# Output of a recurrence kept with its steps on the partitions, its group norm taken along the free axis

## The chip, the cores and the metric

One core of a Trainium2 chip runs the whole program. The metric is the device time of one execution in microseconds (us); a measurement of this kernel can tell about 0.2% (4.7 us) from no change. TensorE does the matrix products, VectorE (DVE in the rows), ScalarE (ACT) and GpSimd (POOL) the rest, SyncE (SP) issues most transfers.

## The reference, cut to what matters

Two layers of a decoder. Every layer has one wide input projection, sliding-window attention on one half of its heads, a recurrence (RWKV-7) on the other half, gates, and an output projection. The change concerns the recurrence's output `ys` for 512 prompt positions and 8 single-step samples, 16 heads of 64 channels:

```python
def step(S, inp):
    r_t, w_t, k_t, v_t, kk_t, a_t = inp
    sa = jnp.einsum('bhij,bhj->bhi', S, -kk_t)
    S = (S * w_t[:, :, None, :] + sa[..., None] * (kk_t * a_t)[:, :, None, :]
         + v_t[..., None] * k_t[:, :, None, :])
    return S, jnp.einsum('bhij,bhj->bhi', S, r_t)
...
mu = jnp.mean(ys, axis=-1, keepdims=True)
var = jnp.mean(jnp.square(ys - mu), axis=-1, keepdims=True)
yn = ((ys - mu) * lax.rsqrt(var + GN_EPS)).reshape(Bn, T, RWKV_WIDTH)
yn = yn * ln_w.astype(f32) + ln_b.astype(f32)
bonus = jnp.sum(r_h * k_h * r_k.astype(f32), axis=-1, keepdims=True) * v_h
y_rw = (yn + bonus.reshape(Bn, T, RWKV_WIDTH)).astype(x.dtype)
```

## The kernel before, in words

All products of a layer form one stream on TensorE: 53 column tiles of the input projection, then 16 of the output projection. A tile takes 96 products of 260 columns (`quarter`, L378; tiles `psP`, `psR`, `psQ`, `psA`, `psO` and so on), each with weights that are split in two parts, `hi` (made on ScalarE, L353) and `lo` (made on VectorE, L363); `lo` is made three quarters of a tile, that is at least 48 products, ahead of its use.

Everything else is written as generators. `Side.tick` is called after each product of the stream and lets at most one generator go on; `yield n` means: go on n products of the stream later. I call the gap between two products of the stream a *place*, and a distance in places is the sum of the numbers that are yielded. So the order of the instructions on every engine is fixed when the program is built, and an engine works through its list strictly from the top.

The recurrence is done by `chain(p, ...)`, once for each of 8 pairs of heads in each of 2 layers, 16 in all; three of them are under way at a time. Its parts, in order:

- the inputs are scaled, and products of queries and keys (`atp`, L636) give the 64x64 matrices `atq`, `atk` of 8 chunks of 64 steps;
- GpSimd inverts 31 steps of triangular 32x32 blocks: it fetches `f` (L660, four transfers) and then does two instructions a step, `tmp` and `xi` (L668, L670);
- blocks are put together: VectorE transposes (`x`, L725), TensorE multiplies them (`t2a`, L731 and L739), with copies by VectorE in between (L734, L743);
- the 8 chunks in turn (tile `seq`): L761 makes both the queries' and the keys' product with the state, of which only the keys' half is read (`rr`, L762); L768 and two copies (`sv`, L769, L770); L772 makes the new state, to which VectorE adds the old one (`mbd`, L779); L773 and L775 add up the output with the channels on the partitions, and ScalarE copies it to `y` (L785);
- the samples' state (`sa`, `st`, `vz`, L793 to L811) and their output (`ys`, L817, L821);
- the group norm of prompt and samples together, over partitions: `y` is split in two parts, a product centres it (`yc`), ScalarE squares it, a second split and product give the variance (`vp`), ScalarE takes the logarithm and the exponential (L840, L841), VectorE scales and adds (L843, L845), the gate `gr` is fetched and multiplied (L849), and the result goes to memory (`yd`, L850).

The tail of pair p runs beside the chunks of pair p+1 and the inversion of pair p+2.

## Time and profile before

| | |
|---|---|
| three runs | 2343.62, 2343.07, 2341.40 us; median 2343.07 |
| the profiled execution | 2344.84 us, of which the span of its instructions is 2343.1 us |
| TensorE, products | busy 2220.5 us of the span, 95% |
| VectorE | busy 1482.1 us, 63% |
| ScalarE | busy 1057.8 us, 45% |
| GpSimd | busy 790.9 us, 34% |
| mean granted TensorE clock | 0.979 of full speed |

The profiled execution lies 1.8 us above the median, and 1.7 us of it lie outside the span. A busy share is an average; TensorE's busy time counts overlapping products once.

### The profile page before, as it was taken

Reading aid. Unit: us, or ns where it says so; the run is one execution under the profiler, and the core shown is the slowest. Engines: PE = TensorE matmul, PEld = TensorE weight load, DVE = VectorE, ACT = ScalarE, POOL = GpSimd, SP = SyncE. Lnnn points to the kernel's source line nnn. Section 1 sums busy time; section 2 is a strip of 40 time slices with the busy share of each in tenths; the row PEclk is TensorE's granted clock in tenths of the full one; section 3 lists DMA queues with packets and bytes.
Section 4 is the critical chain, followed back from the end, with each engine's and each line's share of the span. In section 5 each row is a group of like instructions: output and inputs, shape, how many; then the busy total and the mean of one; then the engine's idle time right before and its main releaser. Section 6 shows DMA issues by size and latency. Waiting matters only on the chain.

```text
span 2343.1 us, 53879 instructions
## 1 busy us (share of the span) xinstructions
PE 2220.5 (95%) x20708; PEld 2094.3 (89%) x20708; DVE 1482.1 (63%) x3712; ACT 1057.8 (45%) x2346; POOL 790.9 (34%) x1412
## 2 busy tenths in 40 slices
PE   5999999999999999999999999999999999999997
PEld 3889989999989898899989998989999999889997
DVE  3465676767885886533376456577766778765445
ACT  3344355545454556422245345344554546553222
POOL 1005656666567000000021516655676430000112
PEclk8999999999999999999999999999999999999998
DMA  9945555333333225777762445543332332144335
GB/s 343 350 160 162 169 168 159 103 90 96 106 91 102 60 78 161 221 239 247 238 215 77 141 149 177 165 123 106 94 96 85 94 93 76 62 132 135 115 116 177
DMA packets 231393, 337.99 MB, mean 144 GB/s; under 512 B 61760, under 2 KB 82368, under 8 KB 230976
## 3 DMA queue, kind: packets, MB, share of 16 engines
q1 hardware_dynamic: 225248, 321.95, 44.3%
q0 software_dynamic: 5888, 12.59, 1.8%
q8 instruction: 163, 2.67, 0.5%
q14 instruction: 94, 0.77, 0.1%
HBM read 303.97 MB, written 32.56 MB: 144 GB/s over the span
## 4 chain that ended last, share of the span: by engine, by line
PE 71%; DVE 12%; DMA 6%; ACT 4%; issue 3%; POOL 3%; SPq 1%; DVEq 0%; ACTq 0%; POOLq 0%
PE psP L378 17%; PE psO L378 14%; PE psA L378 6%; PE psR L378 6%; PE psQ L378 5%; PE psS L378 4%; PE adps L297 4%; DMA rawa<-in_wada_dram 2%; DVE lo L363 2%; PE psK L378 2%; POOL xi L670 1%; PE atp L636 1%; POOL tmp L668 1%; PE seq L772 1%; DMA raw<-in_wout_dram 1%
## 5 line engine op out<-in xcount | busy, mean ns | idle before, releaser
L363 DVE TENSOR_TENSOR lo<-raw,hi 128x512 fp32r<-128x512 f32 x568 | 414.0, 730 | 454.3 <-PE psO L378 133.5
L353 ACT CAST hi<-raw 128x512 fp32r<-128x512 f32 x568 | 350.5, 618 | 628.4 <-PE psP L378 213.5
L378 PE MATMUL psP<-hh,lo 128*128 128x260 f32 x1408 | 307.5, 292 | 0.0
L378 PE MATMUL psP<-hl,hi 128*128 128x260 f32 x1408 | 304.9, 292 | 0.0
L378 PE MATMUL psP<-hh,hi 128*128 128x260 f32 x1408 | 303.8, 292 | 0.2 <-ACT dm L516 0.2
L670 POOL TENSOR_TENSOR xi<-xi,tmp 128x248 f32<-128x248 f32 (+30 forms) x496 | 283.5, 572 | 38.9
L668 POOL TENSOR_TENSOR tmp<-f,xi 128x248 f32<-128x248 f32 (+30 forms) x496 | 257.6, 519 | 85.2 <-DMA f<-d 47.8
L378 PEld LDWEIGHTS psP<-hh,lo 128*128 128x128 f32 x1408 | 225.6, 192 | 6.0 <-issue 4.1
L378 PEld LDWEIGHTS psP<-hl,hi 128*128 128x128 f32 x1408 | 224.9, 192 | 5.9 <-issue 3.3
L378 PEld LDWEIGHTS psP<-hh,hi 128*128 128x128 f32 x1408 | 224.4, 192 | 3.1 <-issue 1.6
L378 PE MATMUL psO<-yh,hi 128*128 128x260 f32 x1024 | 223.5, 284 | 3.6 <-DVE xsn L1191 3.6
L378 PE MATMUL psO<-yh,lo 128*128 128x260 f32 x1024 | 223.2, 284 | 1.7 <-DVE lo L363 1.7
L378 PE MATMUL psO<-yl,hi 128*128 128x260 f32 x1024 | 222.9, 284 | 0.0
L378 PEld LDWEIGHTS psO<-yh,hi 128*128 128x128 f32 x1024 | 165.0, 189 | 5.7 <-issue 5.6
L378 PEld LDWEIGHTS psO<-yh,lo 128*128 128x128 f32 x1024 | 165.2, 189 | 3.6 <-DVE lo L363 1.9
L443 POOL TENSOR_TENSOR rmsr<-rmsv,mhalf 128x3 f32<-128x3 f32 x6 | 5.6, 939 | 476.6 <-DMA raw<-in_wout_dram 444.1
L378 PEld LDWEIGHTS psO<-yl,hi 128*128 128x128 f32 x1024 | 165.0, 189 | 1.6 <-issue 1.6
L1328 POOL TENSOR_SCALAR yo<-xnew,fg 128x260 f32<-128x260 f32 x32 | 31.2, 978 | 392.1 <-DVE xnew L1188 367.9
L297 PE MATMUL adps<-rawa,cT 128*32 128x128 f32 (+1 forms) x2048 | 116.8, 347 | 29.6 <-DMA rawa<-in_wada_dram 29.3
L785 ACT COPY y<-seq 64x64 f32<-64x64 f32 x256 | 52.5, 205 | 194.6 <-DVE mbd L779 135.1
L378 PE MATMUL psQ<-hl,hi 128*128 128x260 f32 x512 | 117.6, 295 | 0.0
L297 PEld LDWEIGHTS adps<-rawa,cT 128*32 128x32 f32 x2048 | 55.2, 114 | 67.2 <-DMA rawa<-in_wada_dram 23.1
(361 smaller groups left out, 5499.9 us busy)
## 6 DMA issues: line engine op xcount, KB each, us to landing
raw<-in_win_dram SPq DMA_DIRECT2D x424, 256.0 KB, 3.3
rawa<-in_wada_dram SPq DMA_DIRECT2D x384, 256.0 KB, 5.0
raw<-in_wout_dram SPq DMA_DIRECT2D x152, 256.0 KB, 3.7
f<-d POOLq DMA_DIRECT2D x64, 128.0 KB, 3.3
gd<-th SPq DMA_DIRECT2D x22, 260.0 KB, 2.6
gr<-gd SPq DMA_DIRECT2D x22, 260.0 KB, 3.8
x<-in_xt_dram SPq DMA_DIRECT2D x16, 260.0 KB, 5.2
yd<-rk SPq DMA_DIRECT2D x16, 260.0 KB, 3.5
```

The costliest lines, as they stand in the source:

```text
L297: pe.matmul(ap[32 * g:32 * g + 32, 0:w], cT[:, kk, :], raw[g * w // 512][:, c:c + w], start=(kk == 0), stop=(kk == KT - 1))
L353: se.copy(out=his[n], in_=raws[n])
L363: ve.tensor_tensor(out=lo, in0=raws.pop(n), in1=hi, op=ALU.subtract)
L378: pe.matmul(ps[:, h, 0:NH], a[:, k % 4], b[:, h * NH:(h + 1) * NH], start=(k == k0 and j == 0), stop=stop)
L443: ge.tensor_tensor(out=r[:, 0:3], in0=v[:, 0:3], in1=mhalf[:, 0:3], op=ALU.pow)
L636: pe.matmul(pss[h][:, e, :], kb[g][hs, e].rearrange("p a t -> p (a t)"), qk[g][hs, e].rearrange("p a t -> p (a t)"), start=True, stop=True)
L668: ge.tensor_tensor(out=tv, in0=f[:, s:s + 1, s + 1:32].to_broadcast([128, 8, 31 - s]), in1=xi[:, :, s:s + 1].to_broadcast([128, 8, 31 - s] ...
L670: ge.tensor_tensor(out=xi[:, :, s + 1:32], in0=xi[:, :, s + 1:32], in1=tv, op=ALU.add)
L772: pe.matmul(mn, kbt[g][:, e], sv[g][:, e], start=True, stop=True)
L785: se.copy(out=y[hs, 64 * c:64 * c + 64], in_=yp[hs, h])
L1328: ge.tensor_scalar(out=out[h][m // 2][:, m % 2], in0=xn[:, h * NH:h * NH + NH], scalar1=fg[:, m:m + 1], scalar2=None, op0=ALU.mult)
```

## The change

The line numbers of the changed kernel are those of before plus 2 to 26.

- Output of a chunk: L761's product already holds the queries' half with the steps on the partitions; ScalarE copies it to `yq` (L777 in the changed kernel). The rest of the output is made with `atq` as the weights, one product of 64 columns for each of the two heads (L791), and copied to `y` (L800). L773 and L775 of before are gone. The weights are read 128 columns wide though only 64 of the results are used; for the last head of a group 72 wide. `atq` has 8 columns more for that, which GpSimd clears.
- GpSimd adds `y` and `yq` (L802).
- Group norm of the prompt: the channels of a head now lie along the free axis, so VectorE takes mean and variance with 8 BN_STATS and 8 BN_AGGR (L812, L815), GpSimd makes the factor and the offset (`rs8`, `mv`, L816 to L820, one of them a power), ScalarE applies them in 8 instructions (L842), four transposes on TensorE bring the channels back to the partitions (`yT`, L855), and VectorE scales and adds (L856).
- Samples: the old way, but on 8 columns alone (L861 to L874, with a power on GpSimd, L870, whose result VectorE reads at L872).
- The last instruction also adds `ln_b` (L875). Factors of one half moved into the parameters (`hrk`, `hln`, `lnw4`).
- Distances: 40 more places ahead of the fetch of `f`; 10, 8 and 4 more in the tail; yields with the sum of 101 places are gone with the norm's old steps. `x1` moved to the shared pool `t2`, which has 72 buffers and not 71.

```diff
@@ -586,7 +588,7 @@
             se.activation(out=rn2, in_=rn2, func=AF.Exp, scale=-0.5)
             ve.tensor_tensor(out=k, in0=k, in1=kr, op=ALU.mult)
             rk = t2([128, N], "rk")
-            ve.scalar_tensor_tensor(out=rk, in0=r, scalar=pc(P_RK), in1=k, op0=ALU.mult, op1=ALU.mult)
+            ve.scalar_tensor_tensor(out=rk, in0=r, scalar=hrk[:, l, p:p + 1], in1=k, op0=ALU.mult, op1=ALU.mult)
             yield W[14]
             kk = rn2
             ve.scalar_tensor_tensor(out=kk, in0=kr, scalar=pc(P_KK), in1=rn2, op0=ALU.mult, op1=ALU.mult)
@@ -623,11 +625,15 @@
 
             yield W[23] // 2
             rks = low(rk, rkh)
-            atq, atk = [], []
+            atq, atk, aqs = [], [], []
             flat = lambda ap: ap.rearrange("p e h t -> p (e h) t")
             d1 = dp.tile([2, 16, 32, 32], F32, tag="d1", name="d1")
             for g in range(2):
-                atq.append(t2([128, 4, 2, 64], "atq"))
+
+                aq = t2([128, 520], "atq")
+                ge.memset(aq[:, 512:520], 0.0)
+                aqs.append(aq)
+                atq.append(aq[:, 0:512].rearrange("p (e h t) -> p e h t", e=4, h=2))
                 atk.append(t2([128, 4, 2, 64], "atk"))
                 pss = [ps1("atp").rearrange("p (x t) -> p x t", t=128) for _ in range(2)]
                 for e in range(4):
@@ -656,6 +662,7 @@
                 b = kb[g].rearrange("p e a t -> p e (a t)")
                 ge.tensor_tensor(out=b, in0=b, in1=pend8[:, 4 * g:4 * g + 4].unsqueeze(2).to_broadcast([128, 4, 128]),
                                  op=ALU.mult)
+            yield 40
             for j in range(4):
                 ge.dma_start(out=f[j:128:4], in_=d1.rearrange("b c s t -> (b c) s t"))
             xi = wk.tile([128, 8, 32], F32, tag="xi", name="xi", bufs=1)
@@ -720,7 +727,7 @@
                                  in_=d2[b, 8 * g:8 * g + 8].rearrange("c j t -> j c t"))
             yield W[28]
 
-            x1 = sm.tile([128, 2, 8, 32], F32, tag="x1", name="x1", bufs=1)
+            x1 = t2([128, 2, 8, 32], "x1")
             for i in range(2):
                 ve.transpose(out=x1[64:96, i], in_=flat(xT[i])[64:96, :, 0:32])
             yield W[29]
@@ -742,7 +749,13 @@
                 o = (64, 96)[i]
                 ve.tensor_copy(flat(xT[i])[64:96, :, 32:64], pa[o:o + 32, 8:16])
             yield W[31]
-            y = t2([128, N], "y")
+
+            y = t2([128, 4, 128], "y")
+            yq = t2([128, 4, 128], "yq")
+            ge.memset(yq[0:64, 0], 0.0)
+            st6 = sm.tile([128, 8, 6], F32, tag="st6", name="st6", bufs=2)
+            mv = sm.tile([128, 8, 2], F32, tag="mv", name="mv", bufs=2)
+            rs8 = sm.tile([128, 8], F32, tag="rs8", name="rs8", bufs=2)
             for c in range(8):
                 if c == 6:
                     st = t2([128, B, 64], "st")
@@ -755,11 +768,13 @@
                 m0, m1 = mbd[p % 2][c % 2], mbd[p % 2][1 - c % 2]
                 ps = ps1("seq")
                 rp, sp, mn = ps[:, 0:128], ps[:, 128:256], ps[:, 256:384]
-                yp = ps[:, 384:512].rearrange("p (h t) -> p h t", h=2)
+                ap = ps[:, 384:512]
+                ys = slice(64 * (c % 2), 64 * (c % 2) + 64)
                 rr = rrs[p % 2]
                 if c:
                     pe.matmul(rp, qk[g][:, e].rearrange("p a t -> p (a t)"), m0, start=True, stop=True)
                     ve.tensor_tensor(out=rr[64:128], in0=rp[64:128], in1=sv[g][64:128, e], op=ALU.add)
+                    se.copy(out=yq[ys, c // 2], in_=rp[0:64])
                     yield W[32] + 4
                 else:
                     ve.tensor_copy(rr[64:128], sv[g][64:128, e])
@@ -770,9 +785,11 @@
                 ve.tensor_copy(sv[g][64:128, e, 64:128], sp[64:128, 64:128])
                 yield W[33] + 4
                 pe.matmul(mn, kbt[g][:, e], sv[g][:, e], start=True, stop=True)
-                pe.matmul(yp, sv[g][:, e], atq[g][:, e], start=True, stop=(c == 0))
-                if c:
-                    pe.matmul(yp, m0, qk[g][:, e, 0].unsqueeze(1).to_broadcast([128, 2, 64]), start=False, stop=True)
+                for h in range(2):
+                    o = 128 * e + 64 * h
+                    w = min(128, 520 - o)
+                    pe.matmul(ap[0:w, 64 * h:64 * h + 64], aqs[g][:, o:o + w], sv[g][:, e, 64 * h:64 * h + 64],
+                              start=True, stop=True)
                 for h in range(2):
                     hs = slice(64 * h, 64 * h + 64)
                     if c:
@@ -780,10 +797,9 @@
                                                 in1=mn[hs, hs], op0=ALU.mult, op1=ALU.add)
                     else:
                         ve.tensor_copy(m1[hs, hs], mn[hs, hs])
-                for h in range(2):
-                    hs = slice(64 * h, 64 * h + 64)
-                    se.copy(out=y[hs, 64 * c:64 * c + 64], in_=yp[hs, h])
+                se.copy(out=y[ys, c // 2], in_=ap[0:64])
                 yield W[34]
+            ge.tensor_tensor(out=y, in0=y, in1=yq, op=ALU.add)
             for h in range(2):
                 sy.dma_start(out=o_sp[l, p, 64 * h:64 * h + 64], in_=m1[64 * h:64 * h + 64, 64 * h:64 * h + 64])
 
@@ -791,7 +807,17 @@
             sa = t2([128, B * 64], "sa")
             sb = lambda ap: ap.rearrange("p (b i) -> p b i", b=B)
             ve.tensor_tensor(out=sb(sa), in0=st, in1=bc(smp[:, 1]), op=ALU.mult)
-            yield W[35]
+            yield W[35] + 10
+            for i in range(8):
+                ve.bn_stats(out=st6[:, i], in_=y[:, i // 2, 64 * (i % 2):64 * (i % 2) + 64])
+            yield 8
+            for i in range(8):
+                ve.bn_aggr(out=mv[:, i], in_=st6[:, i])
+            ge.tensor_scalar(out=rs8, in0=mv[:, :, 1], scalar1=GN_EPS, scalar2=None, op0=ALU.add)
+            ge.tensor_tensor(out=rs8, in0=rs8, in1=mhalf, op=ALU.pow)
+            yield 4
+            ge.tensor_tensor(out=mv[:, :, 0], in0=mv[:, :, 0], in1=rs8, op=ALU.mult)
+            ge.tensor_scalar(out=mv[:, :, 0], in0=mv[:, :, 0], scalar1=-1.0, scalar2=None, op0=ALU.mult)
             sah = t2([128, B * 64], "sah", F32R)
             se.copy(out=sah, in_=sa)
             ve.tensor_tensor(out=st, in0=st, in1=bc(smp[:, 5]), op=ALU.mult)
@@ -810,43 +836,43 @@
                                     op1=ALU.mult)
             ve.tensor_tensor(out=st, in0=st, in1=sb(sa), op=ALU.add)
             sy.dma_start(out=o_ss[l, p], in_=st)
+
+            for i in range(8):
+                yi = y[:, i // 2, 64 * (i % 2):64 * (i % 2) + 64]
+                se.activation(out=yi, in_=yi, func=AF.Identity, scale=rs8[:, i:i + 1], bias=mv[:, i, 0:1])
             yield W[38]
             ps = ps1("ys")
 
             for b in range(0, B, 2):
                 pe.matmul(ps[:, 2 * b:2 * b + 4], st[:, b:b + 2].rearrange("p b i -> p (b i)"),
                           rbd[:, b:b + 2].rearrange("p b h -> p (b h)"), start=True, stop=True)
+            ysm = sm.tile([128, 4, B], F32, tag="ysm", name="ysm", bufs=2)
             for h in range(2):
                 for i in range(2):
-                    ve.tensor_copy(y[64 * h:64 * h + 64, T + i:N:2], ps[64 * i:64 * i + 64, 2 * i + h:2 * B:4])
+                    ve.tensor_copy(ysm[64 * h:64 * h + 64, 0, i:B:2], ps[64 * i:64 * i + 64, 2 * i + h:2 * B:4])
+            ps = ps1("yT")
+            for j in range(4):
+                pe.transpose(ps[:, 128 * j:128 * j + 128], y[:, j], ident)
+            ve.scalar_tensor_tensor(out=b2[:, 0:T], in0=ps, scalar=hln[:, l, p:p + 1], in1=b2[:, 0:T], op0=ALU.mult,
+                                    op1=ALU.add)
             yield W[39]
 
-            yh = high(y)
-            yield W[40]
-            ys = low(y, yh)
-            yield W[41]
-            ycs = t2([128, N], "ycs")
-            s2 = y
-            for h in range(2):
-                se.copy(out=ycs[:, h * NH:(h + 1) * NH], in_=sums(cmat, ys, h, "yc"))
-                yield W[42]
-            se.activation(out=s2, in_=ycs, func=AF.Square)
-            s2h = high(s2)
-            yield W[43]
-            s2s = low(s2, s2h)
-            yield W[44]
-            vps = [sums(bones, s2s, h, "vp") for h in range(2)]
-            for h in range(2):
-                se.activation(out=s2[:, h * NH:(h + 1) * NH], in_=vps[h], func=AF.Ln, bias=bia[:, 0:1])
-            se.activation(out=s2, in_=s2, func=AF.Exp, scale=-0.5)
-            yield W[45]
-            ve.scalar_tensor_tensor(out=s2, in0=ycs, scalar=lnw8[:, l, p:p + 1], in1=s2, op0=ALU.mult, op1=ALU.mult)
-            yield W[46]
-            ve.scalar_tensor_tensor(out=b2, in0=s2, scalar=pc(P_LNB), in1=b2, op0=ALU.add, op1=ALU.add)
+            ps = ps1("yc")
+            pe.matmul(ps[:, 0:B], cmat.bitcast(F32), ysm[:, 0], start=True, stop=True)
+            ve.tensor_copy(ysm[:, 1], ps[:, 0:B])
+            ve.tensor_tensor(out=ysm[:, 2], in0=ysm[:, 1], in1=ysm[:, 1], op=ALU.mult)
             gr = t2([128, N], "gr")
             sy.dma_start(out=gr, in_=gd[l, :, 8 + p])
-            yield W[47]
-            ve.scalar_tensor_tensor(out=b2, in0=b2, scalar=0.5, in1=gr, op0=ALU.mult, op1=ALU.mult)
+            yield W[40]
+            ps = ps1("vp")
+            pe.matmul(ps[:, 0:B], bones.bitcast(F32), ysm[:, 2], start=True, stop=True)
+            ve.tensor_scalar(out=ysm[:, 3], in0=ps[:, 0:B], scalar1=64 * GN_EPS, scalar2=None, op0=ALU.add)
+            ge.tensor_tensor(out=ysm[:, 3], in0=ysm[:, 3], in1=mhalf, op=ALU.pow)
+            yield W[45]
+            ve.scalar_tensor_tensor(out=ysm[:, 1], in0=ysm[:, 1], scalar=lnw4[:, l, p:p + 1], in1=ysm[:, 3],
+                                    op0=ALU.mult, op1=ALU.mult)
+            ve.tensor_tensor(out=b2[:, T:N], in0=b2[:, T:N], in1=ysm[:, 1], op=ALU.add)
+            ve.scalar_tensor_tensor(out=b2, in0=b2, scalar=hln[:, l, 8 + p:9 + p], in1=gr, op0=ALU.add, op1=ALU.mult)
             sy.dma_start(out=yd[l, :, p], in_=b2)
             done_r.append(p)
 
```

What the change does to the order, at three places. The names are tiles, with the buffers' numbers left out; pair 3 is the fourth pair of layer 0, and so on.

GpSimd's list before, where the inversion of pair 3 begins:

```order
L657 TENSOR_TENSOR kb<-kb,pend 128x512 x2
L660 DMA f<-d_5450 32x1024 x4
L662 COPY xi<-cst 128x256
L668 TENSOR_TENSOR tmp<-f,xi 128x248
L670 TENSOR_TENSOR xi<-xi,tmp 128x8x31
```

and now, there and (second piece) some ten steps further on:

```order
L802 TENSOR_TENSOR y<-y,yq 128x512
L663 TENSOR_TENSOR kb<-kb,pend 128x512 x2
L816 TENSOR_SCALAR rs_4794<-mv 128x8
L817 TENSOR_TENSOR rs_4794<-rs_4794,mhalf 128x8
L819 TENSOR_TENSOR mv<-mv,rs_4794 128x8
L820 TENSOR_SCALAR mv<-mv 128x8
L667 DMA f<-d_5474 32x1024 x4
L669 COPY xi<-cst 128x256
```

```order
L677 TENSOR_TENSOR xi<-xi,tmp 128x8x21
L870 TENSOR_TENSOR ysm<-ysm,mhalf 128x8
L675 TENSOR_TENSOR tmp<-f,xi 128x8x20
```

The four instructions of pair 1's `rs8` and `mv` stand ahead of the fetch of pair 3's `f`, and the power for pair 1's samples stands behind step 10 of pair 3's inversion (steps counted from 0). It stands behind step 9 to 12 of another pair's inversion for pairs 1 to 5 of both layers, behind step 30 for pair 0 of layer 1, and inside none for the other five.

VectorE's list before, around the copies (L734) between the two block products of pair 3:

```order
L725 STREAM_TRANSPOSE x_6602<-xT 32x256 x2
L651 TENSOR_TENSOR rk<-bp,v 128x260
L808 TENSOR_TENSOR st<-st,vz 128x512
L809 SCALAR_TENSOR_TENSOR sa<-sab,smp 128x512
L811 TENSOR_TENSOR st<-st,sa 128x512
L651 TENSOR_TENSOR rk<-bp,v 128x260
L363 TENSOR_TENSOR lo<-raw,hi 128x512
L734 COPY x_6602<-t2a 32x256 x2
```

and now (`x` is copied at L741, transposed at L732):

```order
L812 BN_STATS st_5829<-y 128x6 x8
L365 TENSOR_TENSOR lo<-raw,hi 128x512
L514 MEMSET prev 128x1
L517 COPY stash<-psP 128x9
L815 BN_AGGR mv<-st_5829 128x2 x8
L823 TENSOR_TENSOR st<-st,smp 128x512
L824 TENSOR_TENSOR rbd<-smp,hsel 128x16
L732 STREAM_TRANSPOSE x_6753<-xT 32x256 x2
L828 TENSOR_TENSOR sal<-sa,sah 128x512
L829 TENSOR_TENSOR vz<-vz,smp 128x512
L741 COPY x_6753<-t2a 32x256 x2
```

The three sample instructions of pair 2 (`st`, `sa`, `st`) went from between the transposes and the copies to behind them; the statistics of pair 2 and an earlier part of its samples' work now stand ahead.

VectorE's list before, near the end of pair 1:

```order
L845 SCALAR_TENSOR_TENSOR rk<-y,par,rk 128x520
L518 COPY prev<-sstl 128x8
L519 SCALAR_TENSOR_TENSOR v<-prev,par,v 128x520
L779 SCALAR_TENSOR_TENSOR mbd_139<-mbd_140,pend,seq 64x64 x2
L545 TENSOR_TENSOR lws<-lw,lws 128x256
```

and now:

```order
L520 COPY prev<-sstl 128x8
L521 SCALAR_TENSOR_TENSOR v<-prev,par,v 128x520
L872 SCALAR_TENSOR_TENSOR ysm<-ysm,lnw_137 128x8
L874 TENSOR_TENSOR rk<-rk,ysm 128x8
L875 SCALAR_TENSOR_TENSOR rk<-rk,hln,gr 128x520
L547 TENSOR_TENSOR lws<-lw,lws 128x256
L796 SCALAR_TENSOR_TENSOR mbd_140<-mbd_139,pend,seq 64x64 x2
L365 TENSOR_TENSOR lo<-raw,hi 128x512
```

L872 reads what GpSimd's power (L870) makes; right behind it stand the new state of pair 2 (`mbd`), which TensorE needs for the next chunk, and the next `lo`.

## Rows read from the trace of the kernel before

**Rows 1.** The page, part 1: busy us, share of the span, instructions.
```profile
PE 2220.5 (95%) x20708; PEld 2094.3 (89%) x20708; DVE 1482.1 (63%) x3712; ACT 1057.8 (45%) x2346; POOL 790.9 (34%) x1412
```

**Rows 2.** Waits of TensorE: who, for whom, us in total, times, longest.
```profile
PE t2a L739 <- DVE x L734: 14.2, 9, 2.2
PE seq L772 <- DVE sv L770: 12.2, 12, 1.6
PE seq L761 <- DVE mbd L779: 5.8, 6, 1.1
```

**Rows 3.** Timeline of TensorE in three stretches: start, us, what, records merged.
```profile
272.41 0.39 PE L773 MATMUL seq<-atq,sv 128*128 128x128 f32 x2
272.63 0.39 PE L775 MATMUL seq<-qk,mbd 128*128 128x128 f32 x2
...
333.44 0.95 PE L817 MATMUL ys<-rbd,st 128*128 128x4 f32 x8
334.25 0.37 PE L378 MATMUL psP<-hh,lo 128*128 128x260 f32 x1
...
347.85 0.28 PE L418 MATMUL vp<-xhi,sel 128*128 128x260 f32 x1
347.97 0.29 PE L418 MATMUL vp<-xlo,sel 128*128 128x260 f32 x1
```

**Rows 4.** Timeline of ScalarE at the norm's logarithm (pair 1).
```profile
435.27 1.28 ACT L840 ACT_TABLE_LOAD   x1
436.57 0.85 ACT L840 ACTIVATE y<-vp,bia 128x260 f32<-128x260 f32 x2
```

**Rows 5.** Timeline: pair 1's last chunk and end; pair 0's last chunk, layer 1.
```profile
401.34 0.39 PE L768 MATMUL seq<-rr,xT 128*128 128x128 f32 x2
...
450.69 0.70 DVE L849 SCALAR_TENSOR_TENSOR rk<-rk,gr 128x520 f32<-128x520 f32 x1
...
1417.49 0.38 PE L768 MATMUL seq<-rr,xT 128*128 128x128 f32 x2
```

**Rows 6.** Timeline of GpSimd: the inversions of pair 3 (layer 0), pair 1 (layer 1).
```profile
419.27 2.20 POOL L660 DMA_DIRECT2D f<-d  x4 [9.67 <-DMA d<-atk]
...
440.70 0.53 POOL L670 TENSOR_TENSOR xi<-xi,tmp 128x168 f32<-128x168 f32 x1
...
1466.06 0.22 POOL L670 TENSOR_TENSOR xi<-xi,tmp 128x8 f32<-128x8 f32 x1
```

**Rows 7.** Line 443, GpSimd's power: ns min/median/max, first and last start.
```profile
L443 POOL TENSOR_TENSOR rmsr<-rmsv,mhalf x6: 854/885/1262, 21.0 to 2329.3; 128x3 f32<-128x3 f32 x6
```

**Rows 8.** Groups by line and shape, small instructions: busy us, mean ns, idle before.
```profile
L599 POOL COPY smp<-rn 128x8 f32<-128x8 f32 x16 | 7.7, 479 | 99.7 <-DVE rn L592 99.6
L1053 DVE TENSOR_SCALAR ss<-ss,st 128x129 f32<-128x129 f32 x16 | 4.6, 289 | 0.8 <-DMA out_ks_dram<-ktc 0.3
L1052 DVE RECIPROCAL st<-st 128x1 f32<-128x1 f32 x16 | 2.6, 164 | 0.6
```

**Rows 9.** Timeline of VectorE as pair 1 of layer 0 ends.
```profile
441.03 0.17 DVE L515 COPY stash<-psP 128x9 f32<-128x9 f32 x1 [1.93 <-ACT prev L514]
441.23 0.29 DVE L762 TENSOR_TENSOR rr<-seq,sv 64x128 f32<-64x128 f32 x1
...
445.12 0.98 DVE L519 SCALAR_TENSOR_TENSOR v<-prev,par,v 128x520 f32<-128x520 f32 x1
```

**Rows 10.** Timeline of VectorE, then TensorE, around pair 3's block products.
```profile
482.55 0.76 DVE L725 STREAM_TRANSPOSE x<-xT 32x256 f32<-32x256 f32 x2
...
485.01 0.69 DVE L811 TENSOR_TENSOR st<-st,sa 128x512 f32<-128x512 f32 x1
...
486.67 0.87 DVE L734 COPY x<-t2a 32x256 f32<-32x256 f32 x2
...
487.59 0.69 PE L739 MATMUL t2a<-xT,x 32*32 32x32 f32 x32 [1.61 <-DVE x L734]
```

**Rows 11.** One stretch: PE, PEld, DVE, ACT, POOL busy; granted clock; DMA.
```profile
489.00:492.40 3.40, 3.40 (x19) 3.40 (x18) 1.29 (x5) 1.49 (x4) 0.57 (x2) 0.50 0.56 180
```

More of the change, by code (lines that the diff above doesn't have):

```diff
@@ L27 @@
 GN_EPS = 64e-5
-NW2 = 71
+NW2 = 72
 RAWS = 4
@@ L232, in body @@
     bones, cmat, rotm = sel[:, 0], sel[:, 1], sel[:, 2]
-    bia = cpool.tile([128, 1], F32, name="bia")
-    ve.memset(bia, 64 * GN_EPS)
     mhalf = cpool.tile([128, 8], F32, name="mhalf")
@@ L241, in body @@
     oka = cpool.tile([128, L, 8], F32, name="oka")
-    lnw8 = cpool.tile([128, L, 8], F32, name="lnw8")
+    hrk = cpool.tile([128, L, 8], F32, name="hrk")
+    hln = cpool.tile([128, L, 16], F32, name="hln")
+    lnw4 = cpool.tile([128, L, 8], F32, name="lnw4")
     nsk = cpool.tile([128, L, 17], F32, name="nsk")
@@ L252, in derive @@
         ve.tensor_scalar(out=oka, in0=hka, scalar1=-1.0, scalar2=1.0, op0=ALU.mult, op1=ALU.add)
-        ve.tensor_scalar(out=lnw8, in0=par[:, :, P_LNW:P_LNW + 8], scalar1=8.0, scalar2=None, op0=ALU.mult)
+        ve.tensor_scalar(out=hrk, in0=par[:, :, P_RK:P_RK + 8], scalar1=0.5, scalar2=None, op0=ALU.mult)
+        ve.tensor_scalar(out=hln, in0=par[:, :, P_LNW:P_LNW + 16], scalar1=0.5, scalar2=None, op0=ALU.mult)
+        ve.tensor_scalar(out=lnw4, in0=par[:, :, P_LNW:P_LNW + 8], scalar1=4.0, scalar2=None, op0=ALU.mult)
         ve.tensor_scalar(out=nsk, in0=par[:, :, P_SINK:P_SINK + 17], scalar1=-1.0, scalar2=None, op0=ALU.mult)
```

## The prediction

> **What bounds the kernel now.** I read the shares of the page first: TensorE's products cover 95% of the span, VectorE 63%, ScalarE 45%, GpSimd 34% [rows 1]. So a microsecond counts only if TensorE works for it or stands still for it. Then TensorE's waits by what ended them: in the stages of the recurrence they are short waits of 1 to 2 us for VectorE. It waited 14.2 us in 9 places for the copies between the two block products (L739), 12.2 us in 12 places for `sv` (L772), 5.8 us in 6 places for the new state (L761) [rows 2]. The reader is to see that no row there names ScalarE or GpSimd: they cost time only through VectorE. Then the timeline, for prices and for what stands ahead of such a wait.
>
> A place of the stream is longer than one of its products, since chains and other work lie between. From the last chunk's L768 of pair 1 to its L849 the code yields 262 places (13+14+10+4+29+30+13+12+12+4+4+20+12+36+9+40), and the two stand at 401.34 and 450.69 us [rows 5]: 0.188 us a place.
>
> **TensorE's own work.** A float32 product of 128 columns is two records, and the next one starts 0.22 us later; four products of 4 columns (eight records) take 0.81 us, 0.20 us each; a product of the split kind with 260 columns takes 0.12 us [rows 3]. So few columns are hardly cheaper, and a product of 64 columns lies between 0.20 and 0.22. Out per pair: 15 products of L773 and L775 at 0.22, 3.3 us, and eight of `yc` and `vp` at 0.12, 1.0 us: 4.3. In: 16 products of 64 columns, 3.2 to 3.5; two on 8 columns, 0.4; four transposes, each between half such a product and a whole one, 0.4 to 0.9: 4.0 to 4.8. Over 16 pairs between -5 and +8 us; I take **+1**. The halved columns bring nothing, and the seven products saved by the queries' half are spent on splitting the other by heads.
>
> **GpSimd ahead of the inversion, and VectorE's wait for a power.** Before, GpSimd idled 9.67 us ahead of pair 3's `f`, which began at 419.27 us [rows 6], as soon as its source was written. Now four instructions of pair 1 stand ahead of it, and they need pair 1's statistics. In the new order the last L768 comes 40 places later (7.5 us), at about 408.9, and BN_STATS 13+14+20 places (8.8 us) behind that, at 417.7. An instruction of VectorE on one column takes 0.164 us and on 129 columns 0.289 us [rows 8]: 0.22 for BN_STATS on 64 columns, 0.16 for BN_AGGR. Eight of each and the `lo` between them (about 0.7 us, as the equally wide instruction of L811 [rows 10]) are 3.8 us. GpSimd's power is not in the trace at 8 columns; at 3 it takes 0.885 us [rows 7], so 0.9 if it is mostly fixed cost and 2.4 if it goes with the columns; I take 0.9, since a copy on 8 columns takes at most 0.48 us [rows 8] and so little of it is width. The three small ones are between nothing and that copy; I take 0.3 each. So `f` begins 3.8+1.8 = 5.6 us after BN_STATS' place, at 423.3, 4 us later than before.
>
> From `f` to the end of step 10 GpSimd took 22.0 us (419.27 to 441.23) [rows 6], and then comes the power L870: 5.6+22.0+0.9 = 28.5 us after BN_STATS' place, 31.5 with both powers at 2.4. VectorE comes to L872, which needs it, 8+4+4+29+30+13+12+36 = 136 places after BN_STATS: 25.6 us. It is late itself, since L521 (0.98 us [rows 9]) stands just ahead: so it stands still for 1.9 to 4.9 us. What is queued behind: pair 1's last instruction, `lws`, the new state of pair 2, the next `lo`. A `lo` is due 48 places (9 us) on and bears it; the state isn't, TensorE's next chunk asks for it about 23 places (4.3 us) on, and VectorE has some 3 us of work until then. I let 1 us be absorbed and 2.2 us arrive, ten times (pairs 1 to 5 of both layers): **+22**, between 0, if GpSimd has time to spare that I don't see, and 45 (4.5 each).
>
> In the trace an instruction of VectorE that waits does hold the next: L515 stood 1.93 us for ScalarE, and L762 began when it had ended [rows 9]. The Trainium skill says it as a rule (TensorE: Matmul & The Clock Gate, section "Architectural detail: the array is 16× 32×32, not 1× 128×128"): VectorE's queue is strictly first in, first out, and only TensorE may pull weight loads forward. The trace agrees. Were it otherwise, this term and the next would be nothing, and the sum 2348.
>
> Pair 0 of layer 1 fares worse once: its power stands behind pair 1's whole inversion, which ended at 1466.3 us [rows 6]; with 4 us of new work in it and the power itself it ends at 1471.2. L872 is due 40+47+136 places (41.9 us) behind the last L768, which was at 1417.49 [rows 5]: at 1459.4. Of the 11.8 us `lo` bears 9; what is behind it and the scaled inputs of a later pair run late as well: **+6**, between 3 and 10.
>
> **VectorE's bursts.** Before, the three sample instructions stood between transposes and copies: the copies (0.87 us) began at 486.67 behind L811, and TensorE stood 1.61 us [rows 10]. These are moved behind. Now 28 places (5.3 us) from BN_STATS to the first block product hold eight BN_STATS, `lo`, eight BN_AGGR, `st` and the transposes: 1.8+0.7+1.3+0.7+0.8 = 5.3 us, just full. Then `sal`, `vz` and the copies, 0.7+0.7+0.9 = 2.3 us, stand in 7 places (1.3 us): TensorE waits 1 us at every pair, 2 if it comes late to the first. 16 to 32 us against 14.2 now [rows 2]: **+8**, between -14 (all gone) and +18.
>
> **ScalarE** loses two table loads a pair (1.28 us each [rows 4]) and half its copies of `y`. TensorE waits for none of it; it works through VectorE, which stood 1.93 us for a ScalarE that was late in this stretch [rows 9]. Half a us a pair: **-8**, between 0 and -15. The next ACTIVATE starts 0.02 us after its load [rows 4], so 32 loads are 41 us of ScalarE. The Trainium skill (ScalarE: Activation LUTs, section "What ACT_TABLE_LOAD costs") counts about 1.38 us of draining for each switch besides, 85 us in all; the trace shows no such gap, so the measurement decides. By the page's figure the term would be at its end of -15 and the time 7 us lower, an estimate.
>
> **The clock.** After the wait of 1.61 us [rows 10] the granted clock stood at the lower of its levels, 1.2 GHz (0.50), for 3.4 us [rows 11]. Such a stretch costs half its length, 1.7 us. If each of the nine waits at L739 [rows 2] has one, they cost 15 us. Ten new waits and fewer old ones: **+4**, between -15 (all nine gone) and +17 (ten more).
>
> **Sum.** 1+22+6+8-8+4 = +33 us. The profiled execution took 2344.8 us, so 2378; the median of the runs shown lies 1.8 us lower: **2376 us**.
>
> **Hidden, with its cover.** GpSimd's sum of `y` and `yq` runs while it waits for pair 3's `f`. The later inversion is covered by the 40 places. ScalarE's eight scalings have 30 places until the transposes. The gate's fetch keeps 12+36 places.
>
> **Rivals.**
> - *Faster.* The burst leaves the block products and the power is in time. It decides at GpSimd: the power must be done within 26.6 us of BN_STATS' place, so `f` must begin at most 3.7 us behind it. For it: the rows behind L811. Against it: eight BN_STATS and eight BN_AGGR take its room. Then the waits at L739 go down by 12, the clock gives back 10, ScalarE 8, pair 0 of layer 1 and TensorE's work take 7: -23, **2320**.
> - *Twice as slow.* The power goes with its columns, and each new wait takes the clock with it: 45+10+18+17-8+1 = +83, **2426**. Against it: waits of TensorE move it back against GpSimd, so that the next power is less late.
> - *Nothing to measure.* The waits for the power fall where TensorE has `lo` and state in hand, and ScalarE's relief and the moved burst pay for the rest: 2343, within 5 us.
>
> **How the numbers follow.** Forecast 0.46 (own range 2354 to 2402), faster 0.24, twice as slow 0.15, nothing 0.15. 0.2% is 4.7 us, about what a measurement can tell from no change. The forecast and the second rival are slower, with a fifth of the third: 0.64. Faster: the first and a fifth of the third, 0.27; same 0.09. Range 2322 to 2424: half of the first rival and half of the second lie outside.
>
> **What would show it.** Right: GpSimd's idle time ahead of `f` names BN_AGGR; VectorE's wait at L872 names GpSimd's L870, ten times, 2 to 5 us; TensorE's wait at L775 (the old L761) grows from 5.8 us by some 20; BN_STATS near 0.22 us; 64-column products 0.2 us apart. Wrong: a wait at L872 under 1 us, GpSimd's power far from 0.9 us, or waits at L746 (the old L739) gone. Most open is how TensorE's own delays move it against GpSimd: 2 us more of them ahead of L872 halve the largest term.

## The result, and the profile after

The changed kernel took 2358.15 us (median of 4 runs, 2356.51 to 2364.14) against 2343.35 us for the kernel before: ratio 1.0056, 95% interval 1.0035 to 1.0077. That is 14.8 us slower between the medians, 13 by the ratio. The direction was forecast, the size (33 us) was not. The profiled execution took 2356.51 us, with a span of 2354.7 us. The page's first part, busy us and share of the span:

```profile
PE 2220.2 (94%) x20740; PEld 2092.6 (89%) x20740; DVE 1495.8 (64%) x4001; ACT 1003.1 (43%) x2298; POOL 885.1 (38%) x1556
```

TensorE's products are busy for as long as before (2220.2 against 2220.5 us [rows 1]). So all of the 11.6 us by which the span grew are time in which TensorE stands. Its waits (who, for whom, us, times, longest):

```profile
PE seq L787 <- DVE sv L785: 20.0, 18, 2.5
PE seq L775 <- DVE mbd L796: 16.1, 10, 4.8
PE t2a L746 <- DVE x L741: 9.4, 8, 1.9
PE t2a L738 <- DVE x L732: 6.9, 7, 2.1
PE adT L311 <- ACT asb L306: 4.9, 6, 2.9
PE zwa L557 <- DVE lws L547: 3.0, 1, 3.0
PE seq L783 <- ACT yq L777: 2.3, 6, 0.8
```

Against [rows 2]: the wait for the new state (L775, the old L761) rose from 5.8 to 16.1 us, that for `sv` (L787, the old L772) from 12.2 to 20.0. The two waits at the block products together went from 17.6 to 16.3. The new waits behind GpSimd, from the waits of VectorE and of GpSimd:

```profile
DVE ysm L872 <- POOL ysm L870: 19.5, 7, 4.3
DVE st L812 <- POOL y L802: 3.1, 1, 3.1
...
POOL rs L816 <- DVE mv L815: 48.9, 15, 7.4
POOL f L667 <- DMA d<-atk: 34.0, 5, 7.6
```

VectorE stood for the samples' power in seven places. And GpSimd's idle time ahead of `f`, 127.1 us in 16 places before, is down to 34.0 in 5: `rs8` now stands ahead of `f` and waits for BN_AGGR. One such place whole, in the timelines of VectorE, GpSimd and TensorE (near the end of pair 2, layer 0):

```profile
517.23 1.12 DVE L521 SCALAR_TENSOR_TENSOR v<-prev,par,v 128x520 f32<-128x520 f32 x1
522.10 0.42 DVE L872 SCALAR_TENSOR_TENSOR ysm<-ysm,lnw 128x8 f32<-128x8 f32 x1 [3.75 <-POOL ysm L870]
...
523.55 0.66 DVE L547 TENSOR_TENSOR lws<-lw,lws 128x256 fp32r<-128x256 f32 x1
524.22 0.57 DVE L796 SCALAR_TENSOR_TENSOR mbd<-mbd,pend,seq 64x64 f32<-64x64 f32 x2
...
520.39 1.67 POOL L870 TENSOR_TENSOR ysm<-ysm,mhalf 128x8 f32<-128x8 f32 x1
...
520.27 0.28 PE L380 MATMUL psA<-hl,hi 128*128 128x260 f32 x1
524.94 0.77 PE L775 MATMUL seq<-mbd,qk 128*128 128x128 f32 x2 [4.39 <-DVE mbd L796]
```

The reader is to see a chain of three: the power ends at 522.06 us on GpSimd, VectorE's L872 begins, three more instructions stand between it and the new state (L796), and TensorE begins again at 524.94. So 3.75 us of VectorE's wait arrive as 4.39 us at TensorE. The one wait at `zwa` (L557, 3.0 us, at 601.74) comes in the same way behind L872 of the next pair. The clock follows: from 500 to 523.2 us it was granted at 1.00, and in the 6.8 us from 523.20 on, which begin inside this wait, at 0.50, 1.2 GHz (busy us of PE, PEld, DVE, ACT, POOL; granted clock; DMA):

```profile
523.20:530.00 6.80, 5.06 (x23) 5.09 (x24) 2.62 (x6) 3.21 (x8) 5.86 (x13) 0.50 0.22 78
```

VectorE's burst has moved too. At the start of pair 3's chunks (timelines of VectorE and TensorE):

```profile
427.43 0.23 DVE L780 COPY rr<-sv 64x128 f32<-64x128 f32 x1
...
428.20 1.24 DVE L521 SCALAR_TENSOR_TENSOR kr<-prev,par,kr 128x520 f32<-128x520 f32 x1
429.36 1.09 DVE L834 TENSOR_TENSOR st<-st,vz 128x512 f32<-128x512 f32 x1
430.49 0.69 DVE L835 SCALAR_TENSOR_TENSOR sa<-sab,smp 128x512 f32<-128x512 f32 x1
431.21 0.97 DVE L837 TENSOR_TENSOR st<-st,sa 128x512 f32<-128x512 f32 x1
432.21 0.22 DVE L784 COPY sv<-seq 64x64 f32<-64x64 f32 x1
...
432.73 0.49 PE L787 MATMUL seq<-sv,kbt 128*128 128x128 f32 x2 [2.06 <-DVE sv L785]
```

The three sample instructions, which stood ahead of the block products' copies before [rows 10], now stand ahead of the first chunk's `sv`; TensorE waits there instead. The prices, by line and shape (busy us, mean ns, idle before):

```profile
L842 ACT ACTIVATE y<-y,mv,rs 128x64 f32<-128x64 f32 x128 | 44.2, 427 | 5.1 <-POOL mv L820 5.0
L817 POOL TENSOR_TENSOR rs<-rs,mhalf 128x8 f32<-128x8 f32 x16 | 28.5, 1780 | 1.3
L870 POOL TENSOR_TENSOR ysm<-ysm,mhalf 128x8 f32<-128x8 f32 x16 | 27.6, 1726 | 85.5 <-DVE ysm L869 63.9 <-ACT hi L355 21.5
L812 DVE BATCH_NORM_STATS2 st<-y 128x6 f32<-128x64 f32 x128 | 17.6, 208 | 3.1 <-POOL y L802 3.1
```

### The profile page after: what moved, and what is told of

Its sections match the earlier page's. It is cut to its first block, busy times and chain, and to the rows that moved or that the text cites. A ratio compares the mean times of both kernels' runs of the same rounds, so it can differ in the third digit from the quotient of the medians.

```text
span 2354.7 us, 54228 instructions
## 1 busy us (share of the span) xinstructions
PE 2220.2 (94%) x20740; PEld 2092.6 (89%) x20740; DVE 1495.8 (64%) x4001; ACT 1003.1 (43%) x2298; POOL 885.1 (38%) x1556
## 5 line engine op out<-in xcount | busy, mean ns | idle before, releaser
L380 PE MATMUL psP<-hh,lo 128*128 128x260 f32 x1408 | 301.2, 290 | 0.0
L677 POOL TENSOR_TENSOR xi<-xi,tmp 128x248 f32<-128x248 f32 (+30 forms) x496 | 272.5, 549 | 38.9
L675 POOL TENSOR_TENSOR tmp<-f,xi 128x248 f32<-128x248 f32 (+30 forms) x496 | 252.6, 509 | 77.6 <-DMA f<-d 42.0
L299 PE MATMUL adps<-rawa,cT 128*32 128x128 f32 (+1 forms) x2048 | 115.1, 346 | 25.6 <-DMA rawa<-in_wada_dram 25.4
L800 ACT COPY y<-seq 64x128 f32<-64x128 f32 x128 | 33.0, 258 | 229.7 <-DVE mbd L796 160.3
L380 PE MATMUL psQ<-hh,hi 128*128 128x260 f32 x512 | 115.1, 291 | 0.0
```

Source lines behind the costliest of these rows:

```text
L299: pe.matmul(ap[32 * g:32 * g + 32, 0:w], cT[:, kk, :], raw[g * w // 512][:, c:c + w], start=(kk == 0), stop=(kk == KT - 1))
L380: pe.matmul(ps[:, h, 0:NH], a[:, k % 4], b[:, h * NH:(h + 1) * NH], start=(k == k0 and j == 0), stop=stop)
L675: ge.tensor_tensor(out=tv, in0=f[:, s:s + 1, s + 1:32].to_broadcast([128, 8, 31 - s]), in1=xi[:, :, s:s + 1].to_broadcast([128, 8, 31 - s] ...
L677: ge.tensor_tensor(out=xi[:, :, s + 1:32], in0=xi[:, :, s + 1:32], in1=tv, op=ALU.add)
L800: se.copy(out=y[ys, c // 2], in_=ap[0:64])
```

## The experiments

Every ratio is to the kernel before on the same chip, with its 95% interval; differences in us are the difference of ratios times 2346 us, about the median of before in these runs. The columns "busy" (TensorE's products), "stands" (span minus busy) and "clock" (mean granted) are of the one profiled execution. That one is not always typical: in e1 and e10 it was the longest of its kernel (6 and 11 us above the median), in e9 and e18 the shortest (6 us below), and in e15 it lay 5 us below. "S" is the spread version of the changed kernel, explained at its experiment.

| label | kernel | ratio | span | busy | stands | clock |
|---|---|---|---|---|---|---|
| | before | 1 | 2343.1 | 2220.5 | 122.6 | 0.979 |
| | after | 1.0056 | 2354.7 | 2220.2 | 134.5 | 0.980 |
| e1 | after, no power | 0.9939 (0.9918 to 0.9960) | 2338.5 | 2219.9 | 118.6 | 0.980 |
| e2 | after, reader later | 0.9986 (0.9972 to 1.0000) | 2341.5 | 2219.6 | 121.9 | 0.981 |
| e3 | after, norm without GpSimd | 1.0005 (0.9989 to 1.0021) | 2350.5 | 2226.9 | 123.6 | 0.978 |
| e4 | before, 40 ahead of `f` | 0.9908 (0.9888 to 0.9928) | 2321.0 | 2210.5 | 110.5 | 0.987 |
| e5 | after, table loads back | 1.0082 (1.0067 to 1.0097) | 2364.9 | 2228.5 | 136.4 | 0.978 |
| e6 | after, without the 40 | 1.0169 (1.0154 to 1.0184) | 2383.9 | 2242.0 | 141.9 | 0.969 |
| e7 | before, 40 at the start | 0.9875 (0.9858 to 0.9891) | 2319.6 | 2207.6 | 112.0 | 0.988 |
| e8 | S | 1.0113 (1.0095 to 1.0131) | 2373.7 | 2230.0 | 143.7 | 0.975 |
| e9 | before, 16 at the start | 0.9925 (0.9909 to 0.9941) | 2324.4 | 2211.5 | 112.9 | 0.984 |
| e10 | before, 47 at the start | 0.9849 (0.9830 to 0.9868) | 2323.9 | 2218.2 | 105.7 | 0.982 |
| e11 | S, reader later | 0.9937 (0.9918 to 0.9957) | 2332.8 | 2215.1 | 117.7 | 0.985 |
| e12 | e11, 16 at the start | 1.0014 (0.9997 to 1.0032) | 2350.1 | 2220.2 | 129.9 | 0.982 |
| e13 | e11, 47 at the start | 1.0165 (1.0137 to 1.0193) | 2383.1 | 2235.5 | 147.6 | 0.973 |
| e14 | before, 94 at the start | 1.0059 (1.0034 to 1.0084) | 2359.3 | 2226.8 | 132.5 | 0.978 |
| e15 | before, 16 fewer | 1.0041 (1.0026 to 1.0057) | 2351.3 | 2225.2 | 126.1 | 0.979 |
| e16 | e11, 26 for 40 | 1.0010 (0.9996 to 1.0024) | 2350.8 | 2222.2 | 128.6 | 0.982 |
| e17 | e11, the 40 at the start | 0.9933 (0.9916 to 0.9950) | 2329.5 | 2214.4 | 115.1 | 0.985 |
| e18 | before, 70 at the start | 1.0129 (1.0108 to 1.0150) | 2371.6 | 2235.4 | 136.2 | 0.976 |

**The power's wait: e1 and e2.**

```diff
-            ge.tensor_tensor(out=ysm[:, 3], in0=ysm[:, 3], in1=mhalf, op=ALU.pow)
```

> The changed kernel without the power of the samples' norm (L870 is left out, so the samples' output is scaled by the variance and not by its root's inverse); L872 then waits for nothing but VectorE. Theory 1 (VectorE's wait for GpSimd at L872, 19.5 us in 7 times, arrives at TensorE): 2358 minus 15 to 19 us, 2339 to 2343; TensorE's waits at L775 fall from 16.1 us to under 5, the one at L557 (3.0 us) goes. Rival (the wait only takes the place of others, since VectorE's bursts find TensorE less late without it): 2352 to 2358, waits at L787 and at the block products grow by what L775 loses.

```diff
-            yield W[45]
+            yield W[45] + 30
```

> The changed kernel with 30 places (some 5.6 us) more between the power L870 and its reader L872; all work stays. Theory 1 (it is the wait that costs, not the power's time on GpSimd): as without the power, 2339 to 2343, no wait at L872 above 1 us in pairs 1 to 5. Rival (GpSimd's time costs): 2352 to 2358, with the waits at L872 gone all the same.

e1 leaves out one instruction and lies 27 us below the changed kernel; e2 does all the work and lies 16 us below. The waits of TensorE at L775 fell from 16.1 us to 3.0 in e1 and to 1.1 in e2, where VectorE's waits at L872 fell to 3.9 us in 3 places. In both the waits at the block products stayed within 1 us of the changed kernel's (16.4 and 15.5). So the wait does arrive at TensorE, and the rival falls. e2 keeps the power's own time on GpSimd and gets back 16 of 27; the 11 us between them are not taken apart. Nor is what the 30 places do besides: they also move the reader and the two instructions behind it against the stream.

**No GpSimd in the norm: e3.**

```diff
-            ge.tensor_scalar(out=rs8, in0=mv[:, :, 1], scalar1=GN_EPS, scalar2=None, op0=ALU.add)
-            ge.tensor_tensor(out=rs8, in0=rs8, in1=mhalf, op=ALU.pow)
+            ve.tensor_scalar(out=rs8, in0=mv[:, :, 1], scalar1=GN_EPS, scalar2=None, op0=ALU.add)
...
-            ge.tensor_tensor(out=mv[:, :, 0], in0=mv[:, :, 0], in1=rs8, op=ALU.mult)
-            ge.tensor_scalar(out=mv[:, :, 0], in0=mv[:, :, 0], scalar1=-1.0, scalar2=None, op0=ALU.mult)
+            ve.scalar_tensor_tensor(out=mv[:, :, 0], in0=mv[:, :, 0], scalar=-1.0, in1=rs8, op0=ALU.mult,
+                                    op1=ALU.mult)
...
-            ge.tensor_tensor(out=ysm[:, 3], in0=ysm[:, 3], in1=mhalf, op=ALU.pow)
```

e3 leaves out both powers and has VectorE do the other two steps.

> As without the samples' power, and the four GpSimd instructions of the prompt's norm are gone too: VectorE adds the constant and multiplies, both powers are left out (so both parts of the output are scaled by variances). f is then fetched some 3 us earlier. Theory 1 (that delay is hidden): within 4 us of the kernel without the samples' power. Rival (the later inversion costs: kb at L616 stood 8.4 us in 2 times for GpSimd): 5 to 10 us below it.

Neither came: e3 is 15 us slower than e1. Two instructions of VectorE on 8 columns a pair (medians 172 and 165 ns) joined the burst behind BN_AGGR. The waits of TensorE in e3:

```profile
PE seq L787 <- DVE sv L785: 21.8, 18, 2.3
...
PE t2a L746 <- DVE x L741: 10.7, 8, 2.1
PE t2a L738 <- DVE x L732: 9.6, 10, 2.2
```

Against e1 (16.8, 9.4 and 7.0 us) that is 8.9 us for 16 times 0.34 = 5.4 us of work: the interval was full. TensorE's products are busy 7.0 us longer besides (2226.9 against 2219.9 us). The earlier `f` is the other difference of e3, so this reading is argued, not shown by itself.

**The 40 places: e4 and e6.**

```diff
+            yield 40
             for j in range(4):
                 ge.dma_start(out=f[j:128:4], in_=d1.rearrange("b c s t -> (b c) s t"))
```

> The kernel before with the 40 places ahead of the fetch of f and nothing else of the change. Theory 1 (the shift as such is hidden): 2343, within 5 us. Rival (the shift meets other work of TensorE's list and by itself costs or gives a part of the 15 us): 2349 to 2358, or under 2338.

e6 takes the same line out of the changed kernel.

> The changed kernel without the 40 places ahead of the fetch of f. Theory 2 (formed after the kernel before ran 22 us faster with these 40 places alone: they are worth that much here too, and the rest of the change costs 35 us): 2373 to 2386, ratio 1.012 to 1.018. Rival (the 40 places give nothing once the block products' neighbours are changed): ratio 1.003 to 1.008.

Alone, in the kernel before, the line is worth 22 us; in the changed kernel 27 us. In e6 three quarters of it lie in TensorE's products (busy 2242.0 against 2220.2 us). In e4 half of it is time in which TensorE stands (122.6 to 110.5 us), the other half lies in its products: the same 20708 instructions are busy 10.0 us less, at a mean granted clock of 0.987 and not 0.979. e4's waits of TensorE, and VectorE between the two block products of pair 3:

```profile
PE seq L773 <- DVE sv L771: 17.1, 15, 1.8
...
PE t2a L740 <- DVE x L735: 6.6, 10, 1.4
```

```profile
489.86 0.77 DVE L726 STREAM_TRANSPOSE x<-xT 32x256 f32<-32x256 f32 x2
490.66 0.69 DVE L809 TENSOR_TENSOR st<-st,vz 128x512 f32<-128x512 f32 x1
...
491.99 0.69 DVE L812 TENSOR_TENSOR st<-st,sa 128x512 f32<-128x512 f32 x1
492.72 0.87 DVE L735 COPY x<-t2a 32x256 f32<-32x256 f32 x2
493.61 0.74 DVE L363 TENSOR_TENSOR lo<-raw,hi 128x512 fp32r<-128x512 f32 x1
```

In the kernel before two instructions of the bonus (L651) and a `lo` stood in this interval beside the three of the samples, and the copies came 4.12 us behind the transposes' start (482.55 to 486.67 [rows 10]). Here they come 2.86 us behind it, `lo` has gone behind them, and TensorE waited 0.39 us for them, not 1.61.

**Why 40: e7, e9 and e10, then e14, e15 and e18.** All six change one number of the kernel before:

```diff
-            yield W[7]
+            yield W[7] + 40
```

(16, 47, 94, -16 and 70 in the others.) e15 does all the instructions, but with 16 places fewer a part of its values is no longer the recurrence's; only its time is used.

> The kernel before with 40 places more at the very start of a chain instead of ahead of the fetch of f: the whole chain moves against the stream of tiles, but its early part (the products of keys, the bonus) moves along. Theory 2 (the gain of 22 us comes from the early part of the next chain, four instructions of VectorE for atk, atq and the bonus, leaving the block products' interval): here they stay in it, waits at the block products stay near 17 us, ratio 0.996 to 1.004. Rival (it comes from the chain's place against the tiles): ratio 0.988 to 0.993, waits at the block products under 10 us.

> The kernel before with 16 places more at the start of a chain. lo is made after every 24 products of the stream, some 23.5 places; 40 places are 1.7 of these, 16 are 0.7 of one, so against the row of lo both shifts put a chain in the same phase. Theory 3 (the gain of 27 us with 40 places comes from lo no longer standing ahead of the copies between the block products, or of other copies that TensorE waits for): ratio 0.985 to 0.992, waits at the block products under 13 us. Rival (it comes from the place against whole tiles, 94 places, or from mere distance): ratio above 0.995.

> The kernel before with 47 places more at the start of a chain: two full rows of lo, so its phase against a chain is as in the kernel before, and half a tile. Theory 3 (phase of lo): ratio 0.995 to 1.005, waits at the block products 15 to 20 us. Rival (place against whole tiles, or the distance itself): ratio 0.985 to 0.992 as with 40 places.

> The kernel before with 94 places more at a chain's start, the length of one tile of the stream. Theory 4 (phase): the old neighbours are back, ratio 0.995 to 1.004, half-clock stretches of some 60 us in all, as before. Rival (lateness): ratio under 0.985.

> The kernel before with 16 places fewer at a chain's start. Theory 4 (phase): some gain or a few us of loss, ratio 0.988 to 1.004. Rival (lateness): slower by as much as 16 more made it faster, ratio 1.005 to 1.012.

> The kernel before with 70 places more at a chain's start. Theory 4 (a curve with the length of a tile, between 0.985 at 47 and 1.006 at 94): ratio 0.992 to 1.002. Rival (no curve, each shift gives its own chance value): anything from 0.985 to 1.01, outside that range as likely as inside.

Two theories of mine and a rival fell one after the other. The early part of the next chain moves along in e7, and the gain is there all the same (0.9875). The phase against `lo` is in e10 that of before, and e10 is the fastest of all. The later the better: e14 is later still and slower. What is left of what I had named is the chain's place against a tile of the stream, 94 places: over the shifts -16, 0, 16, 40, 47, 70, 94 the ratios are 1.004, 1, 0.9925, 0.9875, 0.9849, 1.013, 1.006. Both 70 and 94 came out above what I had expected. The waits at the block products (both lines) go with the ratio in part: 17.6 us at 0, 15.5 at 16, 12.4 at 40, 12.2 at 47, 20.3 at 70, 18.9 at 94; but they are longest, 24.5 us, at -16, which is less slow than 70.

The traces show that the sum is not one curve. In each layer eight tiles `psQ` of the attention stand in the stream while the last pair is still in its chunks. Layer 0's stretch of them, in the kernel before, in e7 and in e14 (the stretch and its length; busy us and instructions of PE, PEld, DVE, ACT, POOL; granted clock; DMA):

```profile
742.78:906.46 163.68, 153.98 (x1350) 146.47 (x1349) 129.86 (x398) 93.73 (x255) 8.15 (x21) 0.99 0.29 86
733.42:891.84 158.42, 153.17 (x1360) 145.88 (x1359) 131.06 (x403) 95.40 (x261) 13.32 (x33) 1.00 0.30 87
737.59:917.59 180.00, 162.43 (x1414) 154.69 (x1413) 134.60 (x410) 95.60 (x266) 25.59 (x56) 0.96 0.26 78
```

The two stretches together are 328.2 us long in the kernel before, 320.2 with 40 at the start, 352.0 with 70 and 357.0 with 94. In e14 more of the last pair's work stands there (1414 instructions of TensorE and not 1350), TensorE stands for 17.6 us and not 9.7, and the clock is lower. Outside the two stretches, by these single profiled executions, 94 is 12.5 us faster than the kernel before, and 70 is 5 us slower; a part of that is the work that has moved into them. So 0 and 94 are nearly alike only as a sum of two opposite parts, which is no evidence of a period, and lateness does cost, beside the attention. That the place against a tile makes the rest of the curve is argued by elimination and not shown: the rival of e18, that each shift has a value of its own, is not refuted. Which neighbours make it (the copies at a tile's end, L512 to L519, are my guess) was not tried.

**The bursts: e8 and e11.** S delays the samples' work behind BN_AGGR by 28 places and gives each piece of it 13, the distance between two steps of a chunk:

```diff
             yield 4
...
+            yield 28
             se.copy(out=sah, in_=sa)
             ve.tensor_tensor(out=st, in0=st, in1=bc(smp[:, 5]), op=ALU.mult)
...
-            yield W[36]
+            yield 13
...
-            yield W[37]
...
+            yield 13
+            ve.tensor_tensor(out=st, in0=st, in1=vz, op=ALU.add)
+            yield 13
...
-            ve.tensor_tensor(out=st, in0=st, in1=vz, op=ALU.add)
...
-            yield W[38]
+            yield 13
```

(ScalarE's eight scalings, L842, moved to behind `vz`, where the `...` below W[37] stands.)

> The changed kernel with the samples' work behind BN_AGGR delayed by 28 places and cut into pieces of one or two instructions that stand between the steps of the next pair's chunks; all work stays, and the reader L872 comes 19 places later. Theory 1 (bursts of VectorE: 16.3 us of waits at the block products and 20.0 at L787, and the wait for the power, 19.5): waits at the block products under 8 us, at L787 under 12, at L872 under 5, ratio 0.985 to 0.992. Rival (the bursts only move to other waits of TensorE, as they moved from the block products to L787): ratio 0.997 to 1.003, which is the wait for the power alone.

e11 adds `yield W[45] + 40` ahead of the reader.

> The spread version of the changed kernel (the samples' work cut into pieces behind the block products; it ran at 1.011 with 44.2 us of waits for the power at its reader, in 11 times) with the reader 40 places later. All work stays. Theory 1 (the wait for the power arrives at TensorE whole, and the bursts' waits are gone): minus 44 to 55 us, ratio 0.986 to 0.993, under 5 us of waits at the reader. Rival (TensorE would have stood for other things in that time): ratio 1.000 to 1.005.

e8 was slower, and shows what the wait costs. From its waits of VectorE and of TensorE (L873 is the old L872):

```profile
DVE ysm L873 <- POOL ysm L871: 44.2, 11, 6.4
...
PE seq L783 <- ACT yq L777: 29.2, 10, 6.8
...
PE zwa L557 <- ACT sg L558: 15.7, 3, 6.5
```

The waits at the block products are gone. With them went the time that TensorE had lost ahead of L872: the reader is due 17 places later (63 became 80; I had counted 19), but its power is issued as much later, behind more steps of the inversion, and VectorE stood for it in eleven places. The waits behind it carry ScalarE's names, since ScalarE waits for VectorE (at `yq` 137.7 us, 100.1 in the changed kernel). e11, with the reader 40 places later, is 41 us faster than e8, and no wait at the reader is left: theory 1, 3 us short of its range. As in e2, what the 40 places do to the instructions behind the reader is not taken apart.

**The spread version's phase: e12, e13, e16 and e17.** They add 16 or 47 at the start, put 26 in place of 40, or move the 40 to the start.

> The spread version with the late reader, and 16 places more at a chain's start; all work stays. Theory 4 (in the kernel before a chain stands in a bad phase against the stream; the changed kernel's 40 places have left it already): within 8 us of the version without the 16 places, ratio 0.990 to 0.998. Rival (the later a chain, the better): ratio under 0.989.

> As above with 47 places more at a chain's start. Theory 4 (phase): within 8 us of the version without, ratio 0.990 to 0.998. Rival (the later a chain, the better): ratio under 0.985, as the kernel before gained 35 us by 47.

> The spread version with the late reader and 26 places ahead of the fetch of f instead of 40; all work stays. Theory 4 (one curve over the phase, best near 40 to 47): ratio 0.994 to 1.001, a little above the 0.9937 at 40. Rival (the spread kernel has a curve of its own, falling towards fewer places, as 56 and 87 gave 1.001 and 1.017): under 0.990.

> The spread version with the late reader and its 40 places at the chain's start instead of ahead of the fetch of f. Theory 4 (the phase of the chain's later parts counts): within 8 us of the version with them ahead of f, ratio 0.990 to 0.998. Rival (the early part's place counts as well; the kernel before gained 5 us more with the shift at the start): 0.985 to 0.990.

Over the sums 26, 40, 56 and 87 the ratios are 1.0010, 0.9937 (0.9933 with the 40 at the start), 1.0014 and 1.0165: best near 40, and bad where the kernel before is bad. My guess that e12 and e13 would stay within 8 us was wrong; e17 came as expected, e16 at the far end of its range. That fits a phase and does not show one: of the 50 us between the spans of e13 and e11, 17 lie in the two stretches of `psQ`.

**Table loads: e5.**

```diff
+            se.activation(out=tbl, in_=one[:, 0:1], func=AF.Ln)
+            se.activation(out=tbl, in_=tbl, func=AF.Exp, scale=-0.5)
             ps = ps1("vp")
```

> The changed kernel with one logarithm and one exponential on a single column put back ahead of the samples' variance product, so that ScalarE loads its tables about 65 times again and not 33 times; nothing reads the two results. Theory 1 (the relief of ScalarE, 41 us of table loads, is worth some 10 us to TensorE): ratio to the kernel before 1.009 to 1.011 against 1.0056 without. Rival (ScalarE's waits changed through the shift, not through the loads): 1.004 to 1.007.

6 us slower than the changed kernel, between the two; the intervals overlap (from 1.0067, and up to 1.0077), so the size is unclear. The waits for `yq` rose from 2.3 to 7.7 us.

## Why the prediction was right about the direction and wrong about the size

The step that failed is the sentence "The later inversion is covered by the 40 places": the distance was written under "hidden, with its cover" and got no price. It was worth -22 us in the kernel before (e4) and -27 in the changed one (e6 against it). With it the sum is 33 - 22 = 11 us (6 with the 27), against 14.8 measured. Put the other way round, the rest of the change, after against e4, costs 1.0056 - 0.9908 = 0.0148, 35 us, where the six terms gave 33. That these agree to 2 us is partly luck: the two intervals leave about 7 us either way (an estimate), the terms below are off in both directions, and the rest contains shifts of its own in the tail (22 places more, 101 fewer) that no run takes apart. Why the 40 places are worth this much stays open. I had worked out each new wait from what stands in a row on VectorE, but moved everything in a chain from the inversion on against the stream without asking who its new neighbours were.

The terms one by one:

- TensorE's own work, +1: 0 (busy 2220.2 against 2220.5).
- VectorE's wait at L872, +22: right in size (16 to 27 by e2 and e1), wrong in its parts, so the size is partly luck. Forecast were ten waits of 1.9 to 4.9 us; there were seven, 19.5 us. Five of the ten pairs stood over 1 us (one more 0.84), for 1.57 to 4.28 us, and pair 0 of layer 1 for 3.9. (Without the 40 places, in e6, all ten stood, 30.4 us in all.) I had let 1 us of each be absorbed; the five of 3.75, 3.14, 2.03, 4.28 and 1.57 us are followed by waits of TensorE of 4.39, 3.00, 2.09, 4.75 and 2.26. The power takes 1.67 us at the median and not 0.9, which I had named as a sign of being wrong: it lies between my two bounds, 0.9 and 2.4. "Were it otherwise" (VectorE passing a waiting instruction) is out: in e8 VectorE stood 6.4 us. That is the rule of the Trainium skill (TensorE: Matmul & The Clock Gate, section "Architectural detail: the array is 16× 32×32, not 1× 128×128") that VectorE's queue is strictly first in, first out; the trace agrees.
- That TensorE's own delays move it against GpSimd was named as most open, and it fits what is seen: pairs 1 and 4 of layer 0 and 1 and 2 of layer 1 did not wait (0.09 us at most). Pair 1's L872 in layer 0 came at 447.96 us, behind two stands of 2.54 and 2.06 us at L787; in e8, without the waits at the block products, eleven places waited. No run shows it by itself.
- Pair 0 of layer 1, +6: about half, in two places. BN_STATS stood 3.1 us for `y` (L802, inside pair 1's inversion), and TensorE 2.9 at `adT`; at L872 little more reached it.
- Bursts at the block products, +8: -1.3 there, +7.8 at L787. The burst's size was near, its place wrong: eight BN_STATS run in 1.1 us and not 1.8, so the copies were in time, and the samples' three instructions hit the next step.
- ScalarE, -8: -6 by e5, whose interval overlaps with the changed kernel's.
- The clock, +4: the mean did not move (0.979 and 0.980), as two changes cancel: the 40 places raise it to 0.987 (e4), the rest takes that back, at a price of 9.7 us of busy time (2210.5 in e4, 2220.2 after). I had priced it as a term of its own for single waits; over the runs it goes with the standing in the main (0.969 in e6, 0.988 in e7; e10, with the least standing and 0.982, is off).
